# A two-layer decoder trunk on one core: the matrix memory's block output is transposed four stages later, and half of the last memory queries stands ahead of the first attention scores

## The chip, the cores and the metric

The kernel runs on one core of a Trainium2 chip. The metric is the device time of one execution in microseconds (us). The core has five engines with one instruction queue each: TensorE (PE in the rows, with its weight loads as PEld), VectorE (DVE), ScalarE (ACT), GpSimd (POOL) and SyncE (SP), whose queue here issues nearly all transfers. Each engine takes its own instructions in order; engines wait for one another by semaphores.

## What is computed

A sequence of 1024 tokens of width 1024 goes through two layers in float32. Layer 0 is a gated convolution and a chunked spatial gating; layer 1, the place of the change, is multi-head latent attention (8 heads, causal softmax) beside an mLSTM matrix memory (4 heads). Both layers end with an output projection, a SwiGLU feed-forward and a gated per-layer embedding. Cut to what the change touches:

```python
def odd_mixer(hn, ...):
    z = hn @ w_in                       # q_lat, kv_lat, k_pe, mq, mk, mv, mo, gates
    y_c = latent_attention(...)         # 8 heads, softmax(q k^T) v, causal
    h_m = mlstm_chunkwise(mq, mk, mv, i_pre, f_pre)
    y_d = sigmoid(mo) * rmsnorm(h_m, g_mh)
    return concatenate([y_c, y_d]) @ w_out

def step(carry, xs):                    # one chunk of the matrix memory
    c_mat, n_vec, m = carry
    s = einsum('bhtd,bhsd->bhts', qb, kb) * w_intra
    num = einsum('bhts,bhsv->bhtv', s, vb) + w_inter[..., None] * einsum('bhtd,bhvd->bhtv', qb, c_mat)
    den = sum(s, -1) + w_inter * einsum('bhtd,bhd->bht', qb, n_vec)
    h = num / maximum(abs(den), exp(-m_t))[..., None]
    c_new = decay * c_mat + einsum('bhs,bhsv,bhsd->bhvd', w_s, vb, kb)
```

## The kernel before

The kernel is written with tiles and pools that insert the semaphores, and a scheduler settles the order of each engine's instructions when the program is built: the written order is a wish, the built order may differ by some places.

The stretch that matters is the attention of layer 1. Before it, the projections of layer 1 are computed: among them the memory's queries in four parts, `mq_part(g, n, ps)`, g for a pair of heads and n for a half of the tokens. A part is 24 matmuls 128x512 (the tile `mq`), one DVE instruction that scales it out of PSUM (L1522), and two transfers to `mqT_d` in device memory. The parts with g = 0 are done before the attention's pools open; those with g = 1 (n = 0 and 1) in the first turn of the attention loop, after the first scores.

The attention loop runs over 64 units, a unit being a head h and a block b of 128 queries, with b from 7 down to 0. For a unit, PE computes the scores `S` against all keys up to b in three passes of each up to 512 wide piece (L1770, L1771, L1772, and L1774 for the mask); DVE takes the maximum (`nm`, L1779, L1782); ACT the exponential (`P`, L1793); PE transposes `P` by 128x128 pieces (`PT`, L1870); ACT copies that to `PTs` (L1872); PE multiplies with V into `O` (L1828). After a head's last block, DVE scales the head's output (`yp`, L1810). Scores run up to four PSUM banks ahead. PSUM has eight banks: four for `S`, two for `PT`, one for `O`, and one, with the tag "m", for everything of the matrix memory.

The matrix memory runs between these as a generator, `mem_all`: each `yield` ends a stage, and the attention loop calls the next stage once per piece of a unit. A block of 128 tokens (8 blocks, b = 0 to 7) takes these stages, each with a tile in the one "m" bank, so that a stage's matmuls wait until the tile of the stage before has been read out:

- `pe`: the gate matrix, which ACT turns into `W` (L1654, four instructions)
- `pS`: queries times keys, which DVE multiplies into `W` (L1664)
- `mem_out` for the block before: four PE transposes of `ym` into `yT` (L1627), an ACT copy (L1630), and eight POOL instructions that split it into the two halves `y1h` (L1633) and `y1l` (L1634) for the output projection
- `pi` twice: queries times the state, read out by ACT into `num` (L1683)
- `pn` twice: `W` times the values, which DVE adds to `num` (L1699)
- `pc` twice: the state's update, which DVE adds to `cst` (L1710)

Behind the last stage stands the block's tail, mostly on DVE: denominators, squares on POOL into `ym` (L1722) and their sums (`ss`, L1726), a reciprocal root of some ten short instructions (L233 to L244), and four instructions that write the output to `ym` (L1740). `ym`, `W`, `num`, the gate diagonals `dg` and the loaded tiles have one buffer each. The loads of a next block's tiles (`mqT`, `mkT`, `kw`, `mv`, `gs`) go through SP's queue, beside those of the next head's K, Q and V.

Of the kernel before, what the change touches and what calls it, by code (L numbers as in the profile page):

```python
# [324 lines left out]
def trunk(ctx, tc, x, p, positions, g_mix, g_ffn, g_ple, ev_w_in, ev_w_conv, ev_g_v, ev_w_s,  # L325
# [714 lines left out]
    for ch in range(4):  # L1040
# [29 lines left out]
        for n in range(2):  # L1070
# [3 lines left out]
            m = B.pair(bp, "b", n, ch, "mixa")  # L1074
# [444 lines left out]
    def mq_part(g, n, ps):  # L1519
        B.ws_mm(ps, mq_units[g], KT, X[n])  # L1520
        t = B.tmp("mq")
        nc.vector.scalar_tensor_tensor(  # L1522
            out=t, in0=ps, scalar=MDK**-0.5, in1=R[n], op0=ALU.mult, op1=ALU.mult
        )
        c = slice(n * HT, (n + 1) * HT)
        for a in range(2):
            nc.sync.dma_start(mqT_d[:, 2 * g + a, c], t[a * 64 : a * 64 + 64, :])
        return t
# [17 lines left out]
    def psum(tag, name, bufs, shape=(P, HT)):  # L1546
        return pp.tile(list(shape), F32, tag=tag, name=B.name(name), bufs=bufs)

    def load_head(h):
        t = []  # L1550
        for nm, src in (("K", kT_d), ("Q", qT_d)):
            for i in range(2):
                a = tp.tile([QK, T], F32R, tag=f"{nm}{i}", name=B.name(f"{nm}{i}"), bufs=2)
                nc.sync.dma_start(a.bitcast(F32), src[i][:, h, :].bitcast(F32))
                t.append(a)
        return t
# [4 lines left out]
    def load_V(pr):  # L1561
        V[pr] = tp.tile([P, NT, P], F32, tag="V", name=B.name("V"), bufs=2)
        nc.sync.dma_start(
            V[pr], v_d[:, pr * P : (pr + 1) * P].rearrange("(b p) d -> p b d", p=P)
        )
# [58 lines left out]
    def mem_out(b, y):  # L1624
        pt = psum("m", "yT", 1)
        for j in range(MH):
            nc.tensor.transpose(pt[:, j * P : (j + 1) * P], y[:, j, :], ident)  # L1627
        c = slice((b % 4) * P, (b % 4 + 1) * P)
        yT = B.tmp("yT", (P, MH, P))
        nc.scalar.copy(yT.rearrange("p h t -> p (h t)"), pt)  # L1630
        for j in range(MH):
            hi, lo = mixT[b // 4][4 + j]
            nc.gpsimd.tensor_copy(hi[:, c], yT[:, j, :])  # L1633
            nc.gpsimd.tensor_tensor(  # L1634
                out=lo[:, c], in0=yT[:, j, :], in1=hi[:, c].bitcast(F32), op=ALU.subtract
            )

    def mem_all():
# [4 lines left out]
        before = None  # L1643
        for b in range(NT):
# [20 lines left out]
                out=W.rearrange("p h t -> p (h t)"), in0=pS, in1=W.rearrange("p h t -> p (h t)"),  # L1665
                op=ALU.mult,
            )
            if before:
                yield
                mem_out(*before)  # L1670
            nums = []
            for g in range(2):
                yield
# [17 lines left out]
            for g in range(2):  # L1691
                yield
                pn = psum("m", "pn", 1, (P, 2, MDV + 1))
                for a in range(2):
                    h = 2 * g + a
                    nc.tensor.matmul(
                        pn[:, a, :], W[:, h, :], d["mv"][:, h, :], start=True, stop=True
                    )
                nc.vector.tensor_tensor(out=nums[g], in0=pn, in1=nums[g], op=ALU.add)  # L1699
            for g in range(2):  # L1700
                yield
                pc = psum("m", "pc", 1, (MDK, 2, MDV + 1))
                for a in range(2):
                    h = 2 * g + a
                    nc.tensor.matmul(
                        pc[:, a, :], d["kw"][:, h, :], d["mv"][:, h, :], start=True, stop=True
                    )
                for a in range(2):
                    h = 2 * g + a
                    nc.vector.scalar_tensor_tensor(  # L1710
                        out=cst[:, h, :], in0=cst[:, h, :], scalar=dec[0:MDK, b, h : h + 1],
                        in1=pc[:, a, :], op0=ALU.mult, op1=ALU.add,
                    )
# [31 lines left out]
            before = (b, y)  # L1745
# [12 lines left out]
    def att_scores(u):  # L1758
        h, b = u
        K0, K1, Q0, Q1 = heads[h]  # L1760
        t = slice(b * P, (b + 1) * P)
        q0, q1 = Q0[:, t], Q1[:, t]
        nk = (b + 1) * P
        res = []
        mm = nc.tensor.matmul
        w0 = nk if nk <= HT else max(HT - P, nk - HT) if nk == HT + P else HT
        for c0, w in ((0, w0), (w0, nk - w0))[: 1 + (nk > HT)]:
            s = psum("S", "S", 4)
            diag = c0 + w == nk
            mm(s[:, 0:w], q0, K0[:, c0 : c0 + w], start=True, stop=False)  # L1770
            mm(s[:, 0:w], q0, K1[:, c0 : c0 + w], start=False, stop=False)  # L1771
            mm(s[:, 0:w], q1, K0[:, c0 : c0 + w], start=False, stop=not diag)  # L1772
            if diag:
                mm(s[:, w - P : w], identb, maskq, start=False, stop=True)  # L1774
            res.append((s, w))
        nm = []
        for i, (s, w) in enumerate(res):
            m = tp.tile([P, 1], F32, tag=f"nm{i}", name=B.name("nm"), bufs=6)
            nc.vector.tensor_reduce(out=m, in_=s[:, 0:w], axis=AX.X, op=ALU.max, negate=True)  # L1779
            nm.append(m)  # L1780
        if len(nm) == 2:
            nc.vector.tensor_tensor(out=nm[0], in0=nm[0], in1=nm[1], op=ALU.min)  # L1782
        sc_of[u] = (res, nm[0])

    def att_exp(u):
        h, b = u
        if h not in hd:
            hd[h] = tp.tile([P, NT, 2], F32, tag="rs", name=B.name("rsum"), bufs=2)
        res, nm = sc_of[u]
        ex = []  # L1790
        for i, (s, w) in enumerate(res):
            e = B.tmp("P")
            nc.scalar.activation(  # L1793
                e[:, 0:w], s[:, 0:w], AF.Exp, bias=nm, accum_out=hd[h][:, b, i : i + 1]
            )
            ex.append((e, w))
        sc_of[u] = ex

    O = {}
# [37 lines left out]
    def run_lag():  # L1837
        h, b, t, kb0, w = lag.pop()
        pv(h, b, t, kb0, w)
        if b == 0:  # L1840
            head_done(h)
            if h % 2:
                todo.extend([lambda: pair_out(h // 2, 0), lambda: pair_out(h // 2, 1)])

    for i, u in enumerate(units):
        h, b = u
        if b == NT - 1 and h + 1 < H:
            heads[h + 1] = load_head(h + 1)
            if h % 2:
                load_V(h // 2 + 1)  # L1850
        if i == 0:
            att_scores(u)
            att_exp(u)
            ahead = 1
            for n in range(2):
                mq_part(1, n, psum(("O", "m")[n], "mq", 1))
            mem = mem_all()
            next(mem)
        while ahead < len(units) and (
            ahead <= i + 1 or sum(nbank(v) for v in units[i + 1 : ahead + 1]) <= 4  # L1860
        ):
            att_scores(units[ahead])
            ahead += 1
        if i + 1 < len(units):
            att_exp(units[i + 1])
        kb = 0
        for e, w in sc_of.pop(u):
            pt = psum("PT", "PT", 2)
            for j in range(w // P):
                nc.tensor.transpose(pt[:, j * P : (j + 1) * P], e[:, j * P : (j + 1) * P], ident)  # L1870
            t = tp.tile([P, HT], F32, tag="PTs", name=B.name("PTs"), bufs=3)
            nc.scalar.copy(t[:, 0:w], pt[:, 0:w])  # L1872
            if lag:
                run_lag()
            lag.append((h, b, t, kb, w))
            kb += w // P
            if todo and b < NT - 1:
                todo.pop(0)()
            else:
                next(mem, None)  # L1880
# [59 lines left out]
```

## Time and profile before

| what | value |
|---|---|
| time, median of 3 runs | 2507.98 us (2502.91 to 2508.26) |
| the profiled execution | 2521.44 us, of which 2519.4 us from its first to its last instruction |
| TensorE busy | 97% of the span |
| VectorE, ScalarE, GpSimd busy | 62%, 39%, 39% |
| mean granted TensorE clock | 0.98 of full speed |
| attention of layer 1 | from 1398.8 us (first scores) to 1646.9 us (last head's output) |

A busy share of TensorE of 97% is an average: a matmul that runs at half the clock counts as busy for twice as long. The line of the granted clock says which share of full speed the engine had in each fortieth of the span.

### The profile page before, as it was taken

What the parts mean: (1) busy time and instruction counts of PE and PEld (TensorE: products, weight loads), DVE (VectorE), ACT (ScalarE), POOL (GpSimd) and SP (SyncE); (2) the same over time, 40 slices, a digit from 0 to 9 for tenths busy, and PEclk for the clock granted to TensorE, in tenths of its full rate; (3) what the DMA queues carried; (4) which work ended last, traced back from release to release, by engine and by line L of the source; (5) the groups of instructions that cost most, each with busy time, mean ns of one, the idle gap of its engine ahead of it and who ended that gap; (6) DMA issues with size and microseconds to landing.
All of it is one profiled execution on the core that took longest, in us unless ns stands there. A gap on an engine that the chain in (4) does not pass through costs nothing. (4 is left out here: it accounts for less than half of the span.)

```text
span 2519.4 us, 34032 instructions
## 1 busy us (share of the span) xinstructions
PE 2452.2 (97%) x11510; PEld 2025.9 (80%) x11510; DVE 1563.8 (62%) x2879; ACT 986.8 (39%) x1877; POOL 993.0 (39%) x878
## 2 busy tenths in 40 slices
PE   7999998999999999999999999999999999999999
PEld 6878886888888887789888788877788888887877
DVE  6863487544556888776775447548655554697832
ACT  5321343333234545444554345635332332454521
POOL 3451125655642754222221122113566565285400
PEclk9999999999999999999999869999999999999999
DMA  4221543423336767552446633154333333776820
GB/s 147 84 77 49 155 142 108 140 88 105 110 99 236 246 202 257 168 158 82 117 146 177 168 86 104 47 155 134 118 117 112 94 109 100 251 263 195 289 98 38
DMA packets 358687, 350.75 MB, mean 139 GB/s; under 512 B 24012, under 2 KB 249649, under 8 KB 358513
## 3 DMA queue, kind: packets, MB, share of 16 engines
q1 hardware_dynamic: 358016, 348.25, 43.9%
q8 instruction: 90, 1.47, 0.2%
q0 software_dynamic: 464, 0.33, 0.1%
q14 instruction: 85, 0.69, 0.1%
q10 hardware_dynamic: 32, 0.01, 0.0%
HBM read 255.18 MB, written 93.32 MB: 138 GB/s over the span
## 5 line engine op out<-in xcount | busy, mean ns | idle before, releaser
L189 PE MATMUL pd<-acth,hd 128*128 128x512 f32 x616 | 242.3, 393 | 11.5 <-DVE res L723 11.5
L190 PE MATMUL pd<-actl,hd 128*128 128x512 f32 x616 | 241.5, 392 | 0.0
L191 PE MATMUL pd<-acth,ld 128*128 128x512 f32 x616 | 241.4, 392 | 0.0
L259 POOL TENSOR_TENSOR S<-S,sq 128x512 f32<-128x512 f32 x62 | 89.3, 1440 | 257.5 <-ACT sq L257 256.7
L189 PE MATMUL p<-xch,hg 128*128 128x512 f32 x440 | 175.6, 399 | 12.3 <-ACT o L548 10.0
L191 PE MATMUL p<-xch,lg 128*128 128x512 f32 x440 | 174.7, 397 | 0.0
L190 PE MATMUL p<-xcl,hg 128*128 128x512 f32 x440 | 174.4, 396 | 0.0
L191 PE MATMUL p<-xch,lu 128*128 128x512 f32 x440 | 173.0, 393 | 0.0
L189 PE MATMUL p<-xch,hu 128*128 128x512 f32 x440 | 173.0, 393 | 0.0
L190 PE MATMUL p<-xcl,hu 128*128 128x512 f32 x440 | 172.7, 393 | 0.0
L147 DVE TENSOR_TENSOR actl<-ra,acth 128x512 fp32r<-128x512 f32 x154 | 166.3, 1082 | 10.2 <-ACT acth L146 10.1
L189 PEld LDWEIGHTS pd<-acth,hd 128*128 128x128 f32 x616 | 116.8, 190 | 36.7 <-DVE res L723 12.4
L146 ACT CAST hu<-ru 128x512 fp32r<-128x512 f32 x116 | 71.6, 622 | 188.8 <-PE p L190 176.4
L191 PEld LDWEIGHTS pd<-acth,ld 128*128 128x128 f32 x616 | 116.7, 189 | 24.4
L190 PEld LDWEIGHTS pd<-actl,hd 128*128 128x128 f32 x616 | 116.8, 190 | 24.1
L147 DVE TENSOR_TENSOR ld<-rd,hd 128x512 fp32r<-128x512 f32 x110 | 100.8, 916 | 52.8 <-ACT hd L146 52.5
L146 ACT CAST hg<-rg 128x512 fp32r<-128x512 f32 x110 | 68.2, 620 | 158.4 <-PE p L190 132.1
L540 POOL TENSOR_TENSOR act<-act,sg 128x512 f32<-128x512 f32 x60 | 88.5, 1478 | 103.2 <-DVE act L533 103.0
L146 ACT CAST hd<-rd 128x512 fp32r<-128x512 f32 x110 | 68.2, 620 | 143.6 <-PE pd L190 62.7
L147 DVE TENSOR_TENSOR lu<-ru,hu 128x512 fp32r<-128x512 f32 x116 | 114.8, 990 | 15.1 <-ACT hu L146 15.1
L189 PEld LDWEIGHTS p<-xch,hg 128*128 128x128 f32 x440 | 83.9, 191 | 33.6 <-ACT o L548 10.9
L146 ACT CAST acth<-ra 128x512 fp32r<-128x512 f32 x154 | 94.7, 616 | 22.3 <-DMA ra<-act 16.8
(553 smaller groups left out, 6871.2 us busy)
## 6 DMA issues: line engine op xcount, KB each, us to landing
rd<-in_w_down SPq DMA_DIRECT2D x198, 256.0 KB, 3.8
ra<-act SPq DMA_DIRECT2D x154, 256.0 KB, 3.8
rg<-in_w_gate SPq DMA_DIRECT2D x100, 256.0 KB, 3.2
ru<-in_w_up SPq DMA_DIRECT2D x100, 256.0 KB, 2.9
act<-act SPq DMA_DIRECT2D x88, 256.0 KB, 2.0
act<-at SPq DMA_DIRECT2D x66, 256.0 KB, 2.0
rpg<-in_w_ple_gate SPq DMA_DIRECT2D x48, 256.0 KB, 3.0
rwo<-in_ev_w_out SPq DMA_DIRECT2D x32, 256.0 KB, 2.8
```

The lines of the kernel that those rows point to most:

```text
L146: self.nc.scalar.copy(hi, src)
L147: (eng or self.nc.vector).tensor_tensor(out=lo, in0=src, in1=hi.bitcast(F32), op=ALU.subtract)
L189: mm(ps, a[0], b[0], start=first, stop=False, skip_group_check=more)
L190: mm(ps, a[0], b[1], start=False, stop=False, skip_group_check=more)
L191: mm(ps, a[1], b[0], start=False, stop=last, skip_group_check=more)
L259: eng.tensor_tensor(out=st[n], in0=st[n], in1=sq, op=ALU.add)
L540: (nc.vector if last else nc.gpsimd).tensor_tensor(out=t, in0=t, in1=sg[d["i"], key], op=ALU.mult)
```

## The change

`mem_out` of the block before moves from behind the `pS` stage to behind the second `pn` stage, four stages later. And `mq_part(1, 0)`, half of the last memory queries, is written ahead of the first unit's scores; the other half stays behind them.

```diff
@@ -1665,9 +1665,6 @@
                 out=W.rearrange("p h t -> p (h t)"), in0=pS, in1=W.rearrange("p h t -> p (h t)"),
                 op=ALU.mult,
             )
-            if before:
-                yield
-                mem_out(*before)
             nums = []
             for g in range(2):
                 yield
@@ -1697,6 +1694,9 @@
                         pn[:, a, :], W[:, h, :], d["mv"][:, h, :], start=True, stop=True
                     )
                 nc.vector.tensor_tensor(out=nums[g], in0=pn, in1=nums[g], op=ALU.add)
+            if before:
+                yield
+                mem_out(*before)
             for g in range(2):
                 yield
                 pc = psum("m", "pc", 1, (MDK, 2, MDV + 1))
@@ -1849,11 +1849,11 @@
             if h % 2:
                 load_V(h // 2 + 1)
         if i == 0:
+            mq_part(1, 0, psum("O", "mq", 1))
             att_scores(u)
             att_exp(u)
             ahead = 1
-            for n in range(2):
-                mq_part(1, n, psum(("O", "m")[n], "mq", 1))
+            mq_part(1, 1, psum("m", "mq", 1))
             mem = mem_all()
             next(mem)
         while ahead < len(units) and (
```

The built order of PE, before, from the end of head 0 on: the scores of head 1 have begun, `pS` is that of memory block 1, and `yT` the transposes of block 0's output.

```order
L1870 MATMUL PT_13702<-ident,P_13658 128x128
L1828 MATMUL O_13409<-V_13201,PTs_13663 128x64
L1660 MATMUL pS_13652<-mqT_13475,mkT_13477 128x128 x4
L1828 MATMUL O_13409<-V_13201,PTs_13663 128x64
L1828 MATMUL O_13409<-V_13201,PTs_13704 128x64
L1627 MATMUL yT_13668<-ident,ym_13568 128x128 x4
L1677 MATMUL pi_13708<-cst,mqT_13475 128x129 x2
L1770 MATMUL S_13724<-K_3017_13253,Q_3019_13257 128x512
L1771 MATMUL S_13724<-K_3018_13255,Q_3019_13257 128x512
```

The same place of PE in the changed kernel:

```order
L1828 MATMUL O_13409<-V_13201,PTs_13663 128x64 x2
L1770 MATMUL S_13723<-K_3017_13253,Q_3019_13257 128x512
L1771 MATMUL S_13723<-K_3018_13255,Q_3019_13257 128x512
L1772 MATMUL S_13723<-K_3017_13253,Q_3020_13259 128x512
L1660 MATMUL pS_13652<-mqT_13475,mkT_13477 128x128 x4
L1770 MATMUL S_13727<-K_3017_13253,Q_3019_13257 128x256
L1771 MATMUL S_13727<-K_3018_13255,Q_3019_13257 128x256
L1772 MATMUL S_13727<-K_3017_13253,Q_3020_13259 128x256
L1774 LDWEIGHTS identb
L1774 MATMUL S_13727<-maskq,identb 128x128
L1870 MATMUL PT_13741<-ident,P_13689 128x128 x4
L1828 MATMUL O_13409<-V_13201,PTs_13695 128x64
```

The four `yT` transposes are gone from between `pS` and `pi` (the next PE rows are `pi` and four more `PT`); the scores of head 1's third unit and the transposes of its first unit's `P` have come ahead of `pi`. The transposes of `ym_13568` now stand some 20 rows later, behind the second `pn`.

On ACT the same place reads so (- before, + changed; the unchanged `W` rows are the exponentials of memory block 1):

```order
 L1872 COPY PTs_13663<-PT_13660 128x256
+L1793 ACTIVATE P_13689,rsum_13688<-S_13626,nm_13635 128x512
+L1793 ACTIVATE P_13691,rsum_13688<-S_13630,nm_13635 128x512
 L1654 ACTIVATE W_13621<-pe_13617,bb 128x128 x4
-L1872 COPY PTs_13704<-PT_13702 128x128
-L1630 COPY yT_13673<-yT_13668 128x512
-L1793 ACTIVATE P_13698,rsum_13697<-S_13626,nm_13635 128x512
-L1793 ACTIVATE P_13700,rsum_13697<-S_13630,nm_13635 128x512
```

The exponentials of head 1's first unit stood behind the copy of `yT`; they now stand ahead of `W`, and the copy comes twelve ACT rows later.

On DVE at the start of the attention (`mq_13305` before and `mq_13286` after are the same part, g = 1 and n = 0):

```order
 L1587 CAST maskk<-maskf_13215 128x512
+L1522 SCALAR_TENSOR_TENSOR mq_13286<-mq_13261,R_9759 128x512
 L147 TENSOR_TENSOR lwo_0_3817_16236<-rwo_0_3815_16233,hwo_0_3816_16235 128x512
-L1779 TENSOR_REDUCE nm_13270<-S_13261 128x1
-L1779 TENSOR_REDUCE nm_13272<-S_13265 128x1
-L1782 TENSOR_TENSOR nm_13270<-nm_13270,nm_13272 128x1
-L1522 SCALAR_TENSOR_TENSOR mq_13305<-mq_13280,R_9759 128x512
```

The scaling of the part moves ahead of the first unit's maxima. PE's own order at this place is the same in both kernels: all 24 matmuls of the part, and five of the eight triples of the other one, stand ahead of the first scores before as after. SP's order there is unchanged too.

## Rows read from the trace of the kernel before

**Rows 1.** The page: granted TensorE clock in 40 equal slices, in tenths.

```profile
PEclk9999999999999999999999869999999999999999
```

**Rows 2.** DVE's timeline: outputs of heads 0 and 5 (L1810).

```profile
1433.64 0.68 DVE L1810 TENSOR_TENSOR yp<-O,rr 128x512 f32<-128x512 f32 x1
...
1600.40 0.69 DVE L1810 TENSOR_TENSOR yp<-O,rr 128x512 f32<-128x512 f32 x1
```

**Rows 3.** Head 1, heads 2-5: length; PE, PEld, DVE, ACT, POOL busy; clock; DMA.

```profile
1433.64:1490.24 56.60, 54.44 (x223) 46.86 (x224) 19.80 (x66) 20.10 (x59) 10.46 (x24) 0.52 0.20 54
1490.24:1600.40 110.16, 109.49 (x817) 94.76 (x818) 72.69 (x238) 65.25 (x194) 30.39 (x67) 1.00 0.38 107
```

**Rows 4.** Stretches of 2 us where the clock falls and rises, same columns.

```profile
1434.00:1436.00 2.00, 0.88 (x4) 0.73 (x4) 1.70 (x7) 0.00 (x0) 0.00 (x0) 0.53 0.24 70
...
1488.00:1490.00 2.00, 2.00 (x14) 1.74 (x13) 1.62 (x5) 1.16 (x4) 0.61 (x1) 0.81 0.00 0
```

**Rows 5.** PE's timeline there: start, duration, line; idle before and its releaser.

```profile
1430.42 0.39 PE L1772 MATMUL S<-K,Q 96*128 96x512 f32 x1
1430.65 0.34 PE L1770 MATMUL S<-K,Q 96*128 96x384 f32 x1
...
1431.37 0.33 PE L1828 MATMUL O<-V,PTs 128*128 128x64 f32 x2
1431.63 1.16 PE L1660 MATMUL pS<-mqT,mkT 64*128 64x128 f32 x8
1432.71 0.66 PE L1828 MATMUL O<-V,PTs 128*128 128x64 f32 x4
1435.12 1.19 PE L1627 MATMUL yT<-ident,ym 128*128 128x128 f32 x4 [1.75 <-DVE ym L1740]
```

**Rows 6.** ACT's timeline there.

```profile
1430.38 1.14 ACT L1654 ACTIVATE W<-pe,bb 128x128 f32<-128x128 f32 x4 [1.18 <-PE pe L1649]
...
1436.35 0.58 ACT L1630 COPY yT<-yT 128x512 f32<-128x512 f32 x1 [4.46 <-PE yT L1627]
```

**Rows 7.** DVE's timeline there.

```profile
1430.85 0.69 DVE L1779 TENSOR_REDUCE nm<-S 128x1 f32<-128x512 f32 x1 [0.82 <-PE S L1772]
...
1432.96 0.69 DVE L1664 TENSOR_TENSOR W<-pS,W 128x512 f32<-128x512 f32 x1
...
1434.62 1.14 DVE L1740 SCALAR_TENSOR_TENSOR ym<-num,den,gs 128x128 f32<-128x128 f32 x4
```

**Rows 8.** Waits in the attention, 1396 to 1625 us: total, times, longest.

```profile
PE S L1770 <- DMA Q<-qTd: 2.3, 1, 2.3
PE yT L1627 <- DVE ym L1740: 1.8, 1, 1.8
PE pi L1677 <- ACT yT L1630: 0.7, 1, 0.7
PE yT L1627 <- DVE W L1664: 0.7, 1, 0.7
```

**Rows 9.** PE's timeline: two other gaps.

```profile
1381.83 0.40 PE L1285 MATMUL kTt<-ident,k 128*96 128x128 f32 x2 [1.70 <-DVE k L1498]
...
1398.79 0.47 PE L1770 MATMUL S<-K,Q 96*128 96x512 f32 x1 [2.28 <-DMA Q<-qTd]
```

**Rows 10.** Stretches of 5 us with and behind those gaps, same columns.

```profile
1380.00:1385.00 5.00, 3.30 (x19) 2.80 (x19) 2.78 (x7) 2.50 (x3) 1.04 (x1) 1.00 0.90 242
...
1400.00:1405.00 5.00, 5.00 (x16) 3.40 (x15) 2.07 (x4) 1.68 (x5) 0.00 (x0) 0.66 1.10 255
```

**Rows 11.** Tiles yT and ym: ns min/median/max, first and last start.

```profile
L1633 POOL CAST y1h<-yT x32: 282/290/298, 1437.0 to 1616.0; 128x128 fp32r<-128x128 f32 x32
L1634 POOL TENSOR_TENSOR y1l<-yT,y1h x32: 444/453/462, 1437.5 to 1616.6; 128x128 fp32r<-128x128 f32 x32
L1722 POOL TENSOR_TENSOR ym<-num x16: 612/612/613, 1423.8 to 1601.6; 128x256 f32<-128x256 f32 x16
```

**Rows 12.** DVE's timeline: the part of g = 1, n = 0.

```profile
1403.09 0.69 DVE L1522 SCALAR_TENSOR_TENSOR mq<-mq,R 128x512 f32<-128x512 f32 x1
```

## The prediction

> **What bounds the kernel now.** I read the line of the granted clock first. It stands at full speed nearly everywhere, and two neighbouring slices stand lower, at 0.8 and 0.6 [rows 1]; a slice is 63 us long, so these are the stretch from 1386 to 1512 us, the first heads of the attention. Next, the attention cut at the outputs of its heads: outputs are written at 1433.64 us for head 0 and at 1600.40 us for head 5 [rows 2]. Between the outputs of heads 0 and 1 lie 56.60 us at a clock of 0.52. The next four heads take 110.16 us together, 27.54 us each, at a clock of 1.00 [rows 3]. In both stretches PE is busy for over 96% of the time, and DVE, ACT and POOL for less than 70%. So the attention is bound by PE's own rate, and head 1 takes twice as long because TensorE runs at 1.2 GHz instead of 2.4.
>
> The third reading is where the clock falls and rises. From 1434 to 1436 us it averages 0.53, so it fell within the first 0.2 us; from 1488 to 1490 us it averages 0.81, so it rose near 1488.8 us [rows 4]. That is some 54.7 us at half speed. The fourth is what PE did just before the fall: it came to the end of its work (`O` at 1432.71, 0.66 us long) and stood idle for 1.75 us until 1435.12, waiting for DVE to write `ym`, the output of memory block 0 [rows 5]. `ym` comes at the end of DVE's tail, at 1434.62 [rows 7]. Then came a further 0.7 us in which `pi` waited for ACT to copy `yT` out of the one "m" bank [rows 8]. ACT too stood still, 4.46 us for the transposes [rows 6], with head 1's first exponentials queued behind that copy. These waits are nearly all that PE waits for in the whole attention, beside 2.3 us at its start for the first Q from device memory [rows 8].
>
> **The change part by part.** First, the later transposes. They are the same 32 transposes, 8 ACT copies and 64 POOL instructions, and they issue no transfer, so the work itself changes by nothing. What changes is who stands in line behind a late `ym`. In the new order PE has, from the end of head 0's last `O` but one, the following ahead of `pi`. From the old start of the `O` row at 1431.37: two `O`, 0.26 us to the next start and about 0.2 more; three score passes 512 wide at 0.23 each (1430.42 to 1430.65) make 0.69; `pS` 1.08 (1431.63 to 1432.71) [rows 5]. That reaches 1433.6. Three passes 256 wide at half of 0.23 make 0.35, and four transposes of `P` 0.5 to 0.6, since the four of `yT` took 1.19 at half the clock [rows 5]; with mask and one more `O` PE comes to `pi` at about 1434.7.
>
> `pi` needs the "m" bank, so DVE must have multiplied `pS` into `W`. That started at 1432.96 and took 0.69 us [rows 7]; the new order puts one more maximum of 0.69 us (like the one at 1430.85) ahead of it, and `pS` itself ends later, at about 1433.8 with its drain, so `W` is done at about 1434.5. PE thus waits 0 to 0.3 us where it lost 1.75 and 0.7. The ACT rows that move ahead of `W` fit in the 1.18 us that ACT waited there [rows 6], but for some 0.3 us; `pS` needs `W`'s exponentials out of the bank only from 1432.5 on, so that is covered, with about 0.7 us to spare.
>
> What is late next: `ym` is still written at about 1434.6 to 1436 us, and its transposes now come behind the second `pn`, some 4 us of PE work later, so nothing on PE waits for it. Without that cover, the old 1.75 us would be back.
>
> Price of the wait: head 1 falls from 56.60 us to the 27.54 of its successors [rows 3], 29.1 us. The other way to count is half of 54.7 us at half speed, 27.3, plus the idle 1.75 and 0.7 less 0.3: 29.5. I take 29.1.
>
> Then the later blocks. Seven blocks had the old wait ahead of them; in six of these the trace shows only 0.7 us of it [rows 8], so there is little else to gain. What the new place costs: POOL's squares of a block go into `ym`, which has one buffer, so they now wait for the transposes right ahead of them. Two squares at 0.61 us [rows 11] end about 1.2 us behind the transposes, and DVE, in order, stands up to 1.5 us with the next maxima queued behind. The exponentials that hang on these are for a unit that PE reaches some 4 us later, so I cost it at 0.1 us a block; without that cover it is 1.5 us in each of seven blocks, 10 us. `pc` now waits for ACT's copy of `yT` as `pi` did: nothing gained or lost. POOL's eight split instructions, 2.9 us a block (four at 0.29, four at 0.45) [rows 11], come behind the squares and have a block's time to finish.
>
> Second, the earlier query part. PE's built order is the same in both kernels, so the 2.28 us gap at 1398.79 stays [rows 9], with the low clock behind it, 0.66 from 1400 to 1405 us [rows 10]. On DVE one instruction of 0.69 us [rows 12] leaves a place behind the first maxima for an idle one ahead of them; its two transfers are issued earlier, behind all loads of heads 0 and 1 as before. Bounds: nothing, to 0.69 us gained or, if the early writes delay the first Q, about as much lost. I take nothing.
>
> Sum against the profiled execution: 2521.4 - 29.1 + 0.3 + 0.7 = 2493.3 us, 28 less. The median of the runs shown is 13.5 us below that execution, and no view shows where: if profiling adds it evenly, the runs lose the same 28 and come to 2480; if the runs have a shorter stretch of low clock, they lose 28 - 13.5 = 14.5 and come to 2493.5. The runs differ among themselves by 5.4 us, which bounds what such a stretch seems to vary by, so I give 3 us of the 13.5 to it: a gain of 25, **2483 us**.
>
> **The rivals.** (A) The forecast: the fall at 1434 us is gone and none replaces it. For it: the gap ends just as the clock falls, and all later heads, with the same mixture of work, hold 1.00 for 110 us [rows 3].
>
> (B) The low clock does not hang on this wait. Against the forecast speaks that a gap of 1.70 us at 1381.83 [rows 9] left the clock at 1.00 [rows 10]; for it, that the gap of 2.28 us was followed by a fall, and that the one at 1434 was 1.75 and 0.7 us with only four transposes between. Then only the idle time is won, 2.4 us less 1.0 of new waits: 2506.5 us, no change that this measurement can tell (I count as change what is over 0.2%, 5 us). The Trainium skill, page "TensorE: Matmul & The Clock Gate", section "Why this matters for your kernels", warns of idle gaps between matmul bursts that are longer than either of these; by that rule this wait would not have lowered the clock. The trace does not agree with it: the fall stands within the 1.75 us gap. (The two sentences on the page carry no number of the sum.)
>
> (C) Slower: the new wait of POOL's squares, with DVE standing and the "m" bank handed from `pn` to `yT` to `pc` within a few PE rows, opens a gap on PE in a later block, where PE now runs without one. It decides from a gap of about 1.75 us on, since such a one was followed by 54.7 us of low clock. Each head caught costs 56.6 - 27.5 = 29.1 us: one caught gives back the gain (2508 us, no change), two make it 2537. Against it: the estimated waits are 0 to 0.3 us a block on PE, and no later wait in this attention passes 0.7 us [rows 8].
>
> (D) The change does what it says, but the runs had less low clock than the profiled execution: 2493.5 us, as worked out above.
>
> **How the numbers follow.** A with the 2483 us has 0.57 and D 0.19; both are faster: 0.76. B has 0.10, C 0.14, of which 0.04 catches one head and stays within 0.2%. So the chances are 0.76 faster, 0.14 the same, 0.10 slower. A's own range runs from 2474 us (the lowest run, 2502.9, less 29.1) to 2489. The range has to reach to D and B for eight in ten: 2474 to 2510.
>
> **What would show it.** Right: the low slices of the granted clock are gone but for the short one after 1400 us; outputs of heads 0 and 1 lie some 27 to 30 us apart; PE's `yT` and `pi` rows show no wait over 0.5 us; `ym` ends before its transposes by some microseconds; DVE's sums of squares wait for POOL more than before; ACT's wait for `yT` shrinks. Wrong: a stretch at 0.50 anywhere after 1405 us in the attention, or, under B, at the same place with no gap ahead of it. Edit two is right if the first scores still wait about 2.3 us.

## The result and the profile after

| | before | changed |
|---|---|---|
| median of 5 runs | 2507.98 us (2502.91 to 2516.25) | 2492.85 us (2490.75 to 2495.41) |
| profiled execution | 2521.44 us | 2495.41 us |
| mean granted clock there | 0.98 | 0.99 |

The ratio of the times is 0.9932, with a 95% interval of 0.9908 to 0.9957: the changed kernel is faster by 0.7%, 15.1 us. The forecast was 2483 us. Both the size of the gain and the spread need an explanation: before, the runs lie up to 13 us apart, changed, less than 5. Among all executions of the experiments below, one, of 3423.8 us, ran at a mean clock of 0.65 and is left out of the ratios.

The page's line of the granted clock, changed kernel. The two low slices of [rows 1] are gone:

```profile
PEclk9999999999999999999999999999999999999999
```

The head stretches of the changed kernel: head 1, and heads 2 to 5 together (same columns as [rows 3]):

```profile
1439.67:1468.45 28.78, 28.21 (x213) 24.24 (x211) 18.18 (x60) 17.00 (x50) 8.97 (x21) 1.00 0.38 102
1468.45:1577.96 109.51, 108.59 (x813) 93.95 (x812) 72.03 (x237) 64.67 (x190) 28.18 (x62) 1.00 0.41 108
```

Head 1 takes 28.78 us at a clock of 1.00 where it took 56.60 at 0.52; the heads behind it take what they took. PE's timeline at the place of the old gap [rows 5]:

```profile
1436.28 1.16 PE L1660 MATMUL pS<-mqT,mkT 64*128 64x128 f32 x8
1437.36 0.38 PE L1770 MATMUL S<-K,Q 96*128 96x256 f32 x1
...
1437.89 0.61 PE L1870 MATMUL PT<-ident,P 128*128 128x128 f32 x4
1438.33 0.33 PE L1828 MATMUL O<-V,PTs 128*128 128x64 f32 x2
1438.60 0.71 PE L1674 MATMUL pi<-cst,mqT 64*128 64x129 f32 x4
...
1445.40 0.66 PE L1627 MATMUL yT<-ident,ym 128*128 128x128 f32 x4
```

No row of this stretch has a bracket, those left out here included, so PE never stood in it. DVE's four writes of `ym` began at 1438.55 and took 1.13 us; the transposes come at 1445.40, almost 6 us behind their end. What PE waits for in the whole attention, and what DVE and POOL wait for (waits of the changed kernel, 1396 to 1625 us; total, times, longest):

```profile
POOL ym L1722 <- PE yT L1627: 82.3, 7, 16.1
...
DVE ss L1726 <- POOL ym L1722: 7.4, 13, 1.3
...
PE S L1770 <- DMA Q<-qTd: 3.9, 1, 3.9
ACT yT L1630 <- PE yT L1627: 3.5, 7, 0.7
...
PE pi L1674 <- DVE W L1664: 1.4, 2, 0.8
```

Against [rows 8], the wait for `ym` and that of `pi` on ACT's copy are gone, and ACT waits 3.5 us for the transposes where it waited 14.7. The wait for `W` that `yT` had is now `pi`'s, since the first stage behind `pS` takes the "m" bank. POOL's squares now wait for the transposes, and DVE's sums for the squares. The kernel before has that last wait too, but less of it:

```profile
DVE ss L1726 <- POOL ym L1722: 2.2, 4, 0.6
```

One stretch got worse, that of the first Q. PE's timeline there and the clock behind it, changed kernel (5 us windows of PE: busy, clock, DMA share, GB/s), against [rows 9, 10]:

```profile
1401.91 0.77 PE L1770 MATMUL S<-K,Q 96*128 96x512 f32 x1 [3.88 <-DMA Q<-qTd]
```

```profile
1400.00:1405.00 5.00, 3.09 (x7) 0.53 1.15 206
1405.00:1410.00 5.00, 5.00 (x21) 0.79 0.92 244
```

This stretch at half clock began in the wait for Q and ended near 1407.1 us.

### The profile page after: what moved, and what is told of

It reads as the page before. It is cut to its first block, busy times and chain, and to the rows that moved or that the text cites. A ratio compares the mean times of both kernels' runs of the same rounds, so it can differ in the third digit from the quotient of the medians.

```text
span 2493.7 us, 34019 instructions
## 1 busy us (share of the span) xinstructions
PE 2428.1 (97%) x11510; PEld 2004.3 (80%) x11510; DVE 1574.7 (63%) x2879; ACT 988.2 (40%) x1877; POOL 991.7 (40%) x878
```

## The experiments

Each kernel was timed in five rounds in turn with the kernel before. Every batch has its own median of the kernel before: 2506.72 us for the first four, 2505.67 for the next four, 2505.16 for the last. The theory is that the 1.75 us wait for `ym`, with the 0.7 us behind it, lowers TensorE's clock for head 1, and that the gain is that lost clock. The rivals are that the gain is the idle time or the new order itself, that the other edit brings it, or that the clock falls in this stretch for a cause that is not the wait.

### The kernel before once more

The text of the kernel is unchanged. 

> The kernel before, unchanged, to see its granted clock in several executions. Theory D (low clock of varying length): executions without a change differ by their low-clock stretch; a clock of 0.980 (about 100 us at half speed in all) goes with 2519 us, and shorter executions show a higher clock, up to 0.985 at about 2505 us; ratio 1.00. Rival (the profiled execution was longer by something else): the clock is 0.980 in every execution whatever its time.

Measured: 2505.62 us (2502.6 to 2516.95), ratio 0.9999 (0.9976 to 1.0022). This profiled execution took 2503.45 us, 18.0 less than the first one. PE's timeline at the same gap, and the clock in windows of 2 us:

```profile
1436.61 1.03 PE L1627 MATMUL yT<-ident,ym 128*128 128x128 f32 x4 [1.75 <-DVE ym L1740]
1438.31 0.77 PE L1677 MATMUL pi<-cst,mqT 64*128 64x129 f32 x4 [0.68 <-ACT yT L1630]
```

```profile
1438.00:1440.00 2.00, 1.69 (x6) 0.71 0.46 131
1440.00:1442.00 2.00, 2.00 (x10) 0.50 0.03 8
...
1450.00:1452.00 2.00, 2.00 (x11) 0.50 0.00 0
1452.00:1454.00 2.00, 2.00 (x16) 0.88 0.00 0
```

The gap is the same to 0.01 us, but the clock rises again near 1452.5 us. A mean of 0.71 over 2 us is 1.16 us at half clock; then come 12 us at 0.50, and 0.88 adds 0.48: some 13.6 us, where the first execution had 54.7. That is 41.1 us less of half clock for 18.0 us less time, 0.44 us for each, near the 0.5 that a stretch bound by PE would give. Head 1 alone took 39.48 us here against 56.60, 17.1 of the 18.0 us less (window of head 1: length, PE busy, clock, DMA share, GB/s):

```profile
1435.13:1474.61 39.48, 36.92 (x222) 0.83 0.31 78
```

So the same kernel with the same gap has a low stretch whose length differs from execution to execution, and this difference covers 18 of the up to 26 us by which its times spread.

The expectation asked whether time and clock go together over executions. They do: of the twelve, the six from 2502.6 to 2503.9 us have a mean clock of 0.987 or 0.988, those at 2511.59 and 2513.7 us 0.983, and that at 2516.95 us 0.981; all 15 executions of this kernel, in this run and in the batches beside the experiments, that show 0.981 or less took 2515 us or more. The first execution, 2521.44 us at 0.980, is one of these and not one that profiling made longer. (The expectation had put 2505 us at 0.985; it is nearer 0.987.)

### One edit at a time

Only the later transposes (the first two hunks of the change). 

> Edit one alone: the block's output is transposed behind the second pn, and both query parts stay behind the first scores. Forecast's theory (all of the gain comes from this edit, the early part is worth nothing): 15 to 17 us less than before, no stretch at half clock after 1405 us, and the first scores wait some 2.3 us as before. Rival (the edits work together): less than 8 us gained, and a low-clock stretch in head 1.

Only the earlier query part (the last hunk). 

> Edit two alone: half of the last memory queries ahead of the first scores, the transposes where they were. Forecast's theory: no change, within 5 us of before, with the gap of 1.7 us ahead of yT and the low clock behind it still there. Rival (the early part's transfers delay the first Q): 1.5 to 4 us slower, and the first scores wait about 3.9 us instead of 2.3.

Measured: the later transposes alone take 2494.31 us (2488.57 to 2496.96), ratio 0.9938 (0.9917 to 0.9958). The earlier query part alone takes 2507.62 us (2498.74 to 2519.44), ratio 1.0001 (0.9975 to 1.0027). The first gains 12.4 us against its batch, less than the 15 to 17 expected; in it the clock is 1.00 from 1434 to 1442 us and throughout head 1, which takes 28.78 us as in the changed kernel:

```profile
1435.79:1464.57 28.78, 28.21 (x212) 1.00 0.37 102
```

In the second, the gap and the fall are where they were (PE's timeline; windows of 2 us at the fall and the rise):

```profile
1433.40 1.03 PE L1627 MATMUL yT<-ident,ym 128*128 128x128 f32 x4 [1.75 <-DVE ym L1740]
1435.10 1.23 PE L1677 MATMUL pi<-cst,mqT 64*128 64x129 f32 x4 [0.67 <-ACT yT L1630]
```

```profile
1434.00:1436.00 2.00, 1.33 (x6) 0.63 0.42 113
...
1458.00:1460.00 2.00, 2.00 (x17) 0.89 0.08 13
```

Here the low stretch is 23.9 us long (1.48, 22 and 0.44). The whole gain belongs to the later transposes; the other edit brings nothing that can be measured.

The first scores waited 1.50 us for Q with the early part alone, which is against the rival of 3.9 us, and 1.66 us with the later transposes alone. The three profiled executions with just the first part early waited 3.88, 1.50 and 2.95 us (the changed kernel, this one, and the wait put back once), the seven with neither part early 1.42 to 2.28. Whether the early part delays the first Q in some executions stays open; its times show no loss.

### Filling the gap with work that nobody needs

The kernel before keeps its order. Ahead of block 0's transposes, PE writes seven products that are overwritten at once, into the same bank:

```diff
         pt = psum("m", "yT", 1)
+        if b == 0:
+            for _ in range(7):
+                nc.tensor.matmul(
+                    pt, identb, maskk.rearrange("p h t -> p (h t)"), start=True, stop=True
+                )
```

> The kernel before, with seven extra matmuls 128x512 (a constant, written over by the transposes behind them) ahead of the first block's yT transposes, so that PE works for 1.5 us where it waited for ym; every wait and every other instruction is the same. Theory (the idle gap is what drops the clock): no stretch at half clock in head 1, and 13 to 28 us less than before, as much as the late transposes or more. Rival B (the low clock hangs on something else around there): the clock falls all the same, and the time is that of before within 3 us.

Measured: 2495.18 us, ratio 0.994 (0.9917 to 0.9964); its runs lie between 2492.92 and 2498.06 but for the one of 3423.8 us. That is 11.5 us less than before, a little under the 13 to 28 expected. PE's timeline, and a 2 us window:

```profile
1433.64 1.67 PE L1628 MATMUL yT<-maskk,identb 128*128 128x512 bf16 x7 [0.34 <-DVE W L1669]
1435.14 0.93 PE L1632 MATMUL yT<-ident,ym 128*128 128x128 f32 x4
...
1436.75 0.71 PE L1682 MATMUL pi<-cst,mqT 64*128 64x129 f32 x4 [0.67 <-ACT yT L1635]
```

```profile
1436.00:1438.00 2.00, 1.33 (x7) 1.00 0.47 131
```

The transposes start where they started before (1435.12 in [rows 5]), so none of the wait was saved, and yet the kernel gains nearly what the later transposes gain (0.9938). This decides against the rival of the idle time, and against that of the new order: what counts is that PE does not stand. With the order of before and no low clock, head 1's stretch takes 33.2 us (outputs at 1433.57 and 1466.79); the 56.60 us of the first execution were 23.4 more, 0.43 for each of its 54.7 us at half clock.

The same with fourteen transposes of the identity in place of the seven matmuls:

```diff
+        if b == 0:
+            for j in range(14):
+                c = slice(j % 4 * P, (j % 4 + 1) * P)
+                nc.tensor.transpose(pt[:, c], ident, ident)
```

> As the filled gap, but PE is kept busy for some 1.6 us by 14 transposes 128x128 of a constant instead of seven matmuls 128x512. Theory (any work of PE in the gap does): no fall, ratio 0.993 to 0.996. Rival (only matmuls count as work, transposes do not): the clock falls as before, ratio 0.998 to 1.002.

Measured: 2495.66 us (2493.99 to 2498.73), ratio 0.9952 (0.9934 to 0.997). PE's timeline and the window again:

```profile
1433.57 1.75 PE L1629 MATMUL yT<-ident 128*128 128x128 f32 x14 [0.34 <-DVE W L1668]
1435.15 0.86 PE L1631 MATMUL yT<-ident,ym 128*128 128x128 f32 x4
```

```profile
1436.00:1438.00 2.00, 1.33 (x8) 1.00 0.43 131
```

In this place transposes held the clock as well as matmuls did. The Trainium skill, page "TensorE: Matmul & The Clock Gate", section "Part 4: PE-mode transpose", says that the full clock does not engage for transposes; this run does not agree with it for fp32 transposes of 128x128 that stand between matmuls.

Half of the filling: three matmuls in place of seven. 

> As the filled gap, but with three extra matmuls instead of seven, so that PE idles for 0.3 us ahead of them and some 0.8 us behind them, where it idled 1.75 us in one piece. Theory (the length of the idle time decides, and 0.8 us pieces, as later blocks show them, lower nothing): no low clock in head 1, ratio 0.993 to 0.996. Rival (the sum of idle time around there decides, only a third of it is gone): the clock falls in some executions or all, ratio 0.996 to 1.001 and a spread over 12 us.

Measured: 2501.3 us (2490.91 to 2520.09), ratio 0.9991 (0.9963 to 1.0019). PE's timeline, and windows of 2 us:

```profile
1434.97 0.81 PE L1628 MATMUL yT<-maskk,identb 128*128 128x512 bf16 x3 [0.34 <-DVE W L1669]
1436.39 1.02 PE L1632 MATMUL yT<-ident,ym 128*128 128x128 f32 x4 [0.61 <-DVE ym L1745]
1438.09 0.71 PE L1682 MATMUL pi<-cst,mqT 64*128 64x129 f32 x4 [0.68 <-ACT yT L1635]
```

```profile
1438.00:1440.00 2.00, 1.91 (x8) 0.79 0.42 131
1440.00:1442.00 2.00, 2.00 (x10) 0.50 0.04 8
...
1448.00:1450.00 2.00, 2.00 (x15) 0.65 0.00 0
```

My expectation failed here: with no gap longer than 0.68 us the clock still fell, for 10.2 us (0.84, 8 and 1.4). The whole filling has the first and the last of these three gaps (0.34 and 0.67) and no fall, so the 0.61 us between them, shorter than the last, made the difference: the gaps act together. In the same execution a wait of 1.88 us for the first Q, longer than the three together, was followed by no fall. Three of the twelve runs took 2517 us or more, at a mean clock of 0.98, and one took 2490.91 at 0.992: ten of the twelve lie above 2499 us, over all runs of the whole filling but the one outlier, so the half filling leaves the fall in most executions and perhaps spares one or two. The rival that I had written against it, that the idle time around the place adds up, fits at this place; the longest gap alone does not tell whether the clock falls.

### The wait put back once

The changed kernel, but block 0's output is transposed at the old place and all later ones at the new:

```diff
+            if before and b == 1:
+                yield
+                mem_out(*before)
             nums = []
...
-            if before:
+            if before and b > 1:
```

> The changed kernel with only the first block's output transposed at the old place, behind pS; the other seven blocks keep the later place. Theory (one gap in one block makes the low clock): the gap of 1.7 us is back ahead of yT, the clock falls there, and the time is that of before, ratio 0.998 to 1.002, with a spread over executions of over 15 us. Rival (the gain is the sum over eight blocks): seven eighths of it stay, ratio about 0.994 to 0.995.

Measured: 2503.05 us (2498.19 to 2522.1), ratio 0.9992 (0.9973 to 1.0011). PE's timeline, and the windows of 2 us at the fall and the rise:

```profile
1437.15 1.02 PE L1627 MATMUL yT<-ident,ym 128*128 128x128 f32 x4 [1.75 <-DVE ym L1743]
1438.85 0.96 PE L1677 MATMUL pi<-cst,mqT 64*128 64x129 f32 x4 [0.68 <-ACT yT L1630]
```

```profile
1438.00:1440.00 2.00, 1.32 (x6) 0.79 0.39 123
...
1452.00:1454.00 2.00, 2.00 (x15) 0.79 0.00 0
```

This one wait gives the whole gain back, spread and all. The new place of the other blocks brings nothing that can be measured. The low stretch was 13.7 us long here (0.84, 12 and 0.84).

### Dense work behind the fall

The kernel before keeps its gap; behind head 0's last `O` PE does 24 matmuls 128x512 more, into a tile that nobody reads:

```diff
         pv(h, b, t, kb0, w)
+        if (h, b) == (0, 0):
+            f = psum("PT", "fill", 2)
+            for _ in range(24):
+                nc.tensor.matmul(
+                    f, identb, maskk.rearrange("p h t -> p (h t)"), start=True, stop=True
+                )
```

> The kernel before with 24 extra matmuls 128x512 in one row, some 8 us of work behind the gap (a constant that nobody reads). Theory (the low stretch lasts as long as the attention's own mixture happens not to lift the clock; dense matmuls lift it): the low stretch ends within 10 us of the first extra matmul in every execution, so the spread over executions shrinks from 26 us to under 10, and the time is 2500 to 2510 us, the extra work of 5 to 10 us included. Rival (the length is settled otherwise): the stretch stays 17 to 55 us long, the extra work comes on top, 2512 to 2520 us in the median, and the spread stays.

Measured: 2503.58 us (2499.25 to 2508.74), ratio 0.9984 (0.9969 to 1.0). PE's timeline and windows of 2 us:

```profile
1441.55 5.50 PE L1843 MATMUL fill<-maskk,identb 128*128 128x512 bf16 x24
```

```profile
1438.00:1440.00 2.00, 2.00 (x8) 0.61 0.38 117
1440.00:1442.00 2.00, 2.00 (x11) 0.54 0.03 8
1442.00:1444.00 2.00, 2.00 (x11) 1.00 0.00 0
```

The clock was back near 1441.8 us, 3.4 us behind its fall, just as the dense matmuls had begun, so this one profile does not tell whether they raised it. What bears on it are the times, which came out as expected: the twelve runs lie within 9.5 us, where the 24 runs of the kernel before beside them spread over 21 (2497.71 to 2518.89). With the extra work in it, none of the twelve comes near the 2519 and more that a long low stretch makes. The price is the 5.5 us of extra work, which would explain that the median hardly moves.

### Both query parts ahead of the first scores

The changed kernel with `mq_part(1, 1)` moved too, to cover the wait for the first Q:

```diff
-            mq_part(1, 0, psum("O", "mq", 1))
+            for n in range(2):
+                mq_part(1, n, psum(("O", "m")[n], "mq", 1))
             att_scores(u)
...
-            mq_part(1, 1, psum("m", "mq", 1))
```

> The changed kernel with both last query parts written ahead of the first scores. Theory (the gap ahead of the first scores lowers the clock too, for some 3.4 us): the gap shrinks from 1.5 to 3.9 us to under 1 us, no low clock at 1400 us, 2 to 4 us less than the changed kernel, ratio to before 0.9915 to 0.993. Rival (the first Q comes later by as much, or the first scores come 2 us later for nothing): ratio 0.9935 to 0.9945, as for the late transposes alone.

Measured: 2496.45 us (2491.5 to 2500.39), ratio 0.9956 (0.9938 to 0.9973), against 0.9932 (0.9908 to 0.9957) for the change. PE's waits in the attention:

```profile
PE pi L1674 <- DVE W L1664: 1.4, 2, 0.8
PE S L1772 <- DMA Q<-qTd: 1.1, 1, 1.1
PE S L1770 <- ACT P L1793: 1.1, 1, 1.1
```

Two gaps of 1.1 us took the place of one, and in this execution, 2491.5 us and the fastest of the seven, none lowered the clock. The other six took 2494.58 us or more, at mean clocks of 0.988 to 0.991 against 0.992 here, so it may not stand for them. The 2 to 4 us less than the change that I expected did not come: the times show no gain from it.

## Why the prediction was right, and where its size was off

- **The clock, not the idle time, is what the wait costs.** Right, and shown from both sides: filling the gap gives 0.994 while the transposes come no earlier, and the wait put back once gives 0.9992. Rival B, which gave 2506.5 us, is out. The fall within the gap, read from [rows 4], holds for that execution alone: there the clock fell near 1434.1 us, in the gap from 1433.37 to 1435.12 (and not at its end, as the text says under A). In the four later profiles with a 1.75 us gap in front of `yT` the fall came 1.1 to 2.3 us behind the gap's end, when the 0.7 us wait of `pi` had begun; that the pieces behind the gap count too fits this and the half filling. So the reason given against the rule of the Trainium skill, page "TensorE: Matmul & The Clock Gate", section "Why this matters for your kernels", that the fall stands inside the gap, is true of one execution in five. That the traces do not agree with the length of gap that the rule names stays true: no gap at this place passed 1.75 us, and the clock fell at it in all five profiled executions that had it.
- **The new order reaches `pi` as `W` is done.** Right for block 1: no idle time ahead of `pi` at 1438.60. Two later blocks wait there for `W`, 1.4 us together, 0.8 the longest; the text had said no wait over 0.5 at `pi`. They replace one wait for `W` of 0.7 us that `yT` had [rows 8]; the clock stayed at 1.00.
- **Nothing on PE waits for `ym` any more.** Right: almost 6 us between its end and the transposes; the estimate was about 4.
- **Price of the wait, 29.1 us in the profiled execution.** Near it against that execution: head 1 gave 27.8 us (56.60 less 28.78), and the whole execution 26.0 (2521.44 less 2495.41), where the sum had 28. That 27.8 is so near is in part luck, since the new order also moves some of head 1's scores and transposes ahead of head 0's output: head 0's stretch, from the first scores to its output, grew by 2.9 us (34.85 to 37.76), and the low clock alone was worth 23.4 us of head 1, by the filled gap. The attention's start took more too: PE waited 1.6 us longer for the first Q (3.88 against 2.28 us), and the low clock there lasted longer (0.53 and 0.79 in two windows of 5 us are 4.7 and 2.1 us at half clock; before, 0.66 is 3.4). Its end at 1407.1 us is, by the letter, a stretch at 0.50 after 1405 us, which the text had named as a sign of being wrong; it belongs to the wait for Q and not to the change's place.
- **POOL's squares and DVE behind them cost 0.1 us a block.** The mechanism is right: DVE stood 7.4 us in 13 waits, up to 1.3, where it stood 2.2 in 4. On PE no wait answers to it, so the term is about nothing, and rival C (2508 or 2537 us) did not come.
- **The early query part is worth nothing.** Right: 1.0001 (0.9975 to 1.0027) alone.
- **The step that failed is "so I give 3 us of the 13.5 to it".** It took the spread of three runs, 5.4 us, as the bound of how much the low stretch varies. In truth the first execution had the longest one of those profiled: three more with the same gap, and no dense work behind it, had 13.6, 23.9 and 13.7 us of it, and 35 runs of the kernel before spread from 2496.37 to 2522.1 us. An execution with 13.6 us of it took 2503.45 us, 4.5 below the median shown, so the longer low stretch covers all of the 13.5 us by which the first execution lies above it. The other branch, that profiling adds the 13.5 us evenly, has nothing for it: the mean clock goes with the time in all executions of this kernel. So rival D is what happened. It gave 2493.5 us; measured were 2492.85. That it fits to 0.7 us is in part luck, as the sum behind it was 2 us off and the median of the kernel before moves by 2.8 us between batches. Read back, the gain of 15.1 us, less some 1.8 us of idle time (1.8, 0.7 and 0.7 of [rows 8] against 1.4 now), is 13.3 us, or about 30 us at half clock in a typical execution (an estimate, at 0.44; the 11.5 us of the filled gap give 26).

What stays open: why the low stretch lasts 14 us in one execution and 55 in the next, at the same gap and with PE busy throughout. That the attention's mixture of short matmuls and transposes only sometimes lifts the clock is argued, not shown; the narrower spread with dense matmuls behind the fall speaks for it.

## What to carry to other kernels

Read the granted clock by stretches before the busy shares: an engine that is 97% busy may be running at half its rate, and the thing to look for is the small gap just ahead of the fall, with the shorter ones next to it. If a wait of PE can't be removed, move other ready work into it, or even useless work: here 1.7 us of it were worth 0.6% of the kernel. And when one profiled execution lies above the median by more than the runs' spread, profile it again before a stretch of it is priced, since that stretch may be the reason that it lies there.

## What was not expected of the hardware

- A low stretch of the clock, once begun, lasted 10 to 55 us with PE over 90% busy, and its length differed between executions of one kernel, which makes times spread: 2496.37 to 2522.1 us before, 2488.57 to 2496.96 us with the later transposes alone.
- The length of a gap alone does not tell whether the clock falls: a first wait for Q of 1.66 us was followed by a fall, those of 1.42, 1.50 and 1.88 us in other kernels (the filled gap, the earlier query part, the half filling) and one of 1.70 us at 1381.83 [rows 9, 10] were not, and at `yT` three gaps of 0.34, 0.61 and 0.68 us close together were enough.
- Fourteen fp32 transposes in the gap kept the clock at 1.00 as well as seven bf16 matmuls did.
